# SBUF starting places of the fp32r operands in a two-layer DiT trunk: moving at 0 and weights at 64 modulo 128 bytes

## The chip, the core and the metric

The kernel runs on one core of one Trainium2 chip. The metric is device time in microseconds (us), the median of several executions of the same program. The engines are named as the profile names them: PE (TensorE matmuls), PEld (TensorE weight loads, which overlap PE), DVE (VectorE), ACT (ScalarE), POOL (GpSimd), SP (SyncE, which issues most of the DMAs). A matmul has a *moving* operand, which is streamed through the array, and *weights*, which are loaded into it before; both are read from SBUF.

## What is computed

Two layers of a diffusion transformer over 512 latent tokens of width 1024, with 256 context tokens. Layer 0 mixes with attention (four heads global, four heads with a window of 128 and a sink), layer 1 with a Fourier transform over channels and tokens; both end in a gated ConvFFN of width 2816 with a depthwise convolution of three taps. The parts that matter here, cut from the reference:

```python
def conv_ffn(h, w_up, conv_w, conv_b, w_down):
    u = h @ w_up
    up = jnp.pad(u, ((0, 0), (1, 1), (0, 0)))
    u = up[:, :-2] * conv_w[0] + up[:, 1:-1] * conv_w[1] + up[:, 2:] * conv_w[2] + conv_b
    gate, val = jnp.split(u, 2, axis=-1)
    return (jax.nn.silu(gate) * val) @ w_down
...
    for i in range(DEPTH):
...
        if i % 2 == 0:
            a = i // 2
            y, yc = attention_mixers(h, hc, attn_w_in[a], attn_w_out[a], q_norm_g[a], k_norm_g[a], sink[a],
                                     cos, sin, ctx_next)
        else:
            w_f = fourier_w_out[i // 2]
            y = fourier_mix(h) @ w_f
        x = x + g1 * rms_norm(y, norm_g[i, 1])
        h = modulate(rms_norm(x, norm_g[i, 2]), sh2, sc2)
        x = x + g2 * rms_norm(conv_ffn(h, ffn_w_up[i], ffn_conv_w[i], ffn_conv_b[i], ffn_w_down[i]), norm_g[i, 3])
```

## The kernel before

Almost every large product is made of three matmuls on fp32r tiles. `split` (line 124) turns an fp32 tile into a high part (ACT, a cast) and a low part (DVE or POOL, the difference), and `mm3` (lines 101 to 105) issues high times high, high times low and low times high into the same PSUM tile. So in the profile nearly all matmuls carry the lines L102, L103 and L104, and they are told apart by their tiles: `mm<-hl,wh` has `hl` moving and `wh` as weights. A matmul streams 256 or 512 columns (a few 258 or 384) against weights of 128 by 128.

The tiles that matter:

- `hh`, `hl` (8 x 512 columns): the current activations, high and low. They move in the projections of the FFNs; they are the weights in the attention projections and in the Fourier transform over channels.
- `wh`, `wl` (five buffers each, from `wpair`): the split weights of the matrix that is just being applied. In the projections that give tokens by channels they are the moving side.
- `xh`, `xl` (four buffers each, from `Pairs.pair`): mostly the gated FFN activations, which move in the down projections; at two places they hold weights instead (the output projection's last four blocks and the first up blocks of both FFNs).
- `zh`, `zl` (four buffers each, from `Pairs.spare`): the differences and sums of activation blocks that move in `seven_products`, a scheme of seven block products in place of eight; near the end of each FFN they hold weights of the down projection.
- `qh`, `ql`, `kh`, `kl`, `th`, `tl`: queries, keys and transposed probabilities in attention. `ch`, `cl`: the context's activations.
- `ct`, `Z`, `A`, `B`, `N`: the cosine table, the transformed activations and the outputs of the Fourier mixing. Rows of `ct`, `A` and `N` are 258 columns long.

Tiles live in pools. A pool lays them out in the order in which their names first occur, each rounded up to 32 bytes, and a new pool's tiles wait for the last users of whatever lay in their bytes before. So the starting place of a tile follows from the sizes of all tiles ahead of it, and the order of `mk` calls is also the order in SBUF. The instructions of each engine run in the order of the program; the order itself is set by the code and by priorities, not by places.

`rstd` (line 187) makes the reciprocal root of a mean square in small tiles `st_v`, `st_t`, `st_r`. `tables(0)` casts the first half of the cosine table, on ACT, during the boundary between the layers.

Of the kernel before, what the change touches and what calls it, by code (L numbers as in the profile page):

```python
# [10 lines left out]
F32 = mybir.dt.float32  # L11
F32R = mybir.dt.float32r
# [7 lines left out]
P = 128  # L20
D = 1024
KC = D // P
T = 512
TT = T // P
# [24 lines left out]
SWEEP = [3, 6]  # L49
GP = [1, 1]  # L50
BP = [4, 1]

WARM = 36
HOT = [5, 8, 5, 6]
# [25 lines left out]
def kernel(ctx: ExitStack, tc: tile.TileContext, a):  # L80
# [5 lines left out]
    def mk(pool, shape, dt=F32, tag=None, bufs=1):  # L86
        cnt[0] += 1
        n = nbufs.setdefault((id(pool), tag), (pool, bufs))[1]
        return pool.tile(shape, dt, tag=tag, name=f"{tag}_{cnt[0]}", bufs=n)
# [39 lines left out]
    cp = ctx.enter_context(tc.tile_pool(name="cp", bufs=1))  # L129
# [18 lines left out]
    ident = con[:, K_ID:K_ID + P]  # L148
    ones32 = mk(cp, [P, 32], F32, "ones32")
    V.memset(ones32, 1.0)  # L150
    eps = mk(cp, [P, 1], F32, "eps")
    once = mk(cp, [P, 1], F32, "once")
    V.memset(eps, EPS)
    mods = mk(cp, [P, 2, 6, KC], F32, "mods")
    der = mk(cp, [P, 2, 4, KC], F32, "der")
    scol = mk(cp, [P, 2, KC], F32, "scol")

    def ng(l, i):
        return cols[:, C_NG + (l * 4 + i) * KC:C_NG + (l * 4 + i + 1) * KC]
# [13 lines left out]
    W4 = HT // 4  # L173
# [12 lines left out]

    def rstd(ps):
        w = ps.shape[1]
        v, t, r = (mk(cp, [P, W4], F32, "st_" + c, 2)[:, :w] for c in "vtr")
        S.activation(out=r, in_=ps, func=AF.Abs_reciprocal_sqrt, bias=eps, scale=1.0 / D)  # L190
        V.tensor_scalar(out=v, in0=ps, scalar1=1.0 / D, scalar2=EPS, op0=ALU.mult, op1=ALU.add)
        V.tensor_tensor(out=t, in0=r, in1=r, op=ALU.mult)
        V.scalar_tensor_tensor(out=t, in0=t, scalar=-0.5, in1=v, op0=ALU.mult, op1=ALU.mult)
        V.scalar_tensor_tensor(out=v, in0=t, scalar=1.5, in1=r, op0=ALU.add, op1=ALU.mult)
        return v
# [351 lines left out]
    def out_weights(u, xp):  # L547
        r = raw([P, KC, 256], a["w_out"][u])
        ws = []
        for i in range(2):  # L550
            wh, wl = (xp.pair if u >= 2 else wpair)([P, KC, P])
            split(wh, wl, r[:, :, i * P:(i + 1) * P])
            ws.append([(wh[:, k, :], wl[:, k, :]) for k in range(KC)])
        return ws


    with ExitStack() as es:
# [7 lines left out]
        nsink = mk(ap, [P, 4], F32, "nsink")  # L565
        qst = mk(ap, [P, 2, TT, 2], F32, "qst")
        qtm = mk(ap, [P, 8], F32, "qtm")
        qrs = mk(ap, [P, 2, TT, 2], F32, "qrs")


        kh = mk(ap, [P, NK], F32R, "kh")
        kl = mk(ap, [P, NK], F32R, "kl")

        def keys(kv, parts):
            b0 = 0
# [512 lines left out]
        return ps, sl  # L1088


    class Pairs:
        def __init__(self, es):
            self.first = es.enter_context(tc.tile_pool(name="x0", bufs=1, reuse_waits="tile"))
# [7 lines left out]

        def spare(self, shape):
            return mk(self.pool, shape, F32R, "zh", 4), mk(self.pool, shape, F32R, "zl", 4)

    def up_weights(l, pairs, fis, eng=V):
        for fi in fis:
            r = raw([P, 2, KC, P], a["w_up"][l, fi])
            for i in range(2):
                wh, wl = pairs([P, KC, P])
                split(wh, wl, r[:, i, :, :], eng)  # L1110
                yield [(wh[:, k, :], wl[:, k, :]) for k in range(KC)]
# [120 lines left out]
    def ffn(l, xp, ready, pre, mid, gem, plain=None):  # L1232
# [69 lines left out]
        def begin(us):  # L1302
            for u in us:
                fi, i = divmod(u, 2)
                if u >= len(ready):
                    ready.extend(up_weights(l, xp.pair if u >= 4 and l == 0 else wpair, [fi]))
                first.append((fi, i, ready[u], mk(pps, [P, T], F32, "mm", 6) if plain is None or u < skew else None))

        def sweep(us, sl, ks=range(KC)):
# [69 lines left out]
        for gi, (f0, nch) in enumerate(GROUPS[l]):  # L1379
            end = gi == len(GROUPS[l]) - 1  # L1380
            for fi in range(max(f0, FIRST), f0 + nch):
                if fi == SUMS[l]:
                    bs = seven_inputs(xp)
                if fi in SEVEN[l]:
                    cc = [conv(fi, i, u, None, i == 1) for i, u in enumerate(seven_products(l, fi, pps, bs))]
                else:
                    cc = []
                    for i, w in enumerate(up_weights(l, wpair, [fi])):
                        ps = mk(pps, [P, T], F32, "mm", 6)
                        up_mm(ps, w, slice(0, T))  # L1390
                        cc.append(conv(fi, i, ps))
                gated(fi, cc[0], cc[1], f0)
                if l == 0 and fi not in SEVEN[l]:
                    pump(gem, GP[0])
                if l:
                    pump(down, DOWN.get(fi, 0))
            pump(down, 100)
            if l and end:
                xT = mk(cp, [P, KC, T], F32, "xT")
                SY.dma_start(out=xT, in_=away)  # L1400
            g_ = [gs[fi] for fi in range(f0, f0 + nch)]
            if l and not end:
                down = down_tiles(gi, nch, g_)
                pump(down)
                continue
            ws = {}

            def part(d, hs, ps=None):
                down_part(gi, ws[d], g_, d, hs, ps, end)

            def weights(d):
                ws[d] = down_weights(gi, nch, d, xp.spare if end and 4 <= d < 7 else wpair)


            hs = {d: [0, 1] if not end or d == 0 else [0] for d in range(KC)}
            begun = {}
            if end:
                pump(gem, 100)
                fence()
            keep = dict(fences)  # L1420
            fences.clear()
            for d in range(2):
                weights(d)
            fences.update(keep)
            for d in range(2):
                begun[d] = y_mm(pps, ws[d], g_, hs[d], False)[0]
            for d in range(KC):
                if d not in ws:
                    weights(d)
                part(d, hs[d], begun.get(d))  # L1430
                if gem is not None and not end:
                    pump(gem, GP[1])
            if end:
                mid(ys)
                for d in range(1, KC):
                    part(d, [1])
# [12 lines left out]
    with ExitStack() as es:  # L1449
        up = es.enter_context(tc.tile_pool(name="up", bufs=1, reuse_waits="tile", side="right"))  # L1450
        M1 = 258
        A = [mk(up, [P, 4, M1], F32R, "A%d" % i) for i in range(2)]
        B = [mk(up, [P, 4, 256], F32R, "B%d" % i) for i in range(2)]
        N = [mk(up, [4, M1], F32R, "N%d" % i) for i in range(2)]
        wk = es.enter_context(tc.tile_pool(name="wk", bufs=1, reuse_waits="tile", side="right"))
        zs = ExitStack()
        zp = zs.enter_context(tc.tile_pool(name="zp", bufs=1, reuse_waits="tile"))
        ft = wpair([P, 2, 256])
        st = wpair([P, TT, 256])
        ct = [mk(zp, [P, TT, M1], F32R, "ct%d" % i) for i in range(2)]  # L1460
        split(ft[0], ft[1], raw([P, 2, 256], a["dft_c"]), G)
        lc = raw([P, TT, M1], a["dft_lc"])
        ls = raw([P, TT, 256], a["dft_ls"])
        Z = [mk(zp, [P, TT, 4, 256], F32R, "Z%d" % i) for i in range(2)]


        def over_channels(g, h):
# [130 lines left out]
        group(3, [2, 3])  # L1598
        zs.close()
        xp = Pairs(ctx)  # L1600
        soon = up_weights_dma(1, xp.pair, [0, 1])

        ys = YStat(wk, 2)
        for d in range(KC):
# [140 lines left out]
```

## Time and profile before

| | |
|---|---|
| median of 3 runs | 1145.2 us (1142.97 to 1145.88) |
| span of the profiled execution | 1141.3 us |
| PE busy | 1113.0 us, 98% of the span |
| PEld busy | 965.9 us, 85% |
| DVE busy | 899.9 us, 79% |
| ACT busy | 595.6 us, 52% |
| POOL busy | 177.9 us, 16% |

The span runs from the first to the last instruction that the profile shows in one execution; the timed runs are 1.7 to 4.6 us longer. Matmuls are pipelined: the profile gives each a start and a modelled end, so one matmul's duration overlaps the next one's, and how fast PE goes is read from the distance between starts. Lines of the timeline view read: start in us, duration in us, engine, source line, operation, out<-in, shapes, count.

### The profile page before, as it was taken

To read this page: it belongs to the slowest core of one execution; us is meant where nothing else is said; L and a number is where in the kernel's file an instruction comes from. 1 tells how busy PE (TensorE), PEld (TensorE's weight loads), DVE (VectorE), ACT (ScalarE), POOL (GpSimd) and SP (SyncE) were. 2 spreads that over 40 slices of the span, in tenths; PEclk is the share of its full clock that TensorE was granted. 3 is DMA by queue.
4 is the path that set the end of the run, shared out by engine and by line. 5 is a ranking of instruction groups with operands and counts; after the bars stand their busy time and mean duration, and the time that the engine had idled before them with its cause. 6 is when DMAs were issued, how large, how long until landed. Compare 5 with 4: busy or idle time off the path is not lost.

```text
span 1141.3 us, 19565 instructions
## 1 busy us (share of the span) xinstructions
PE 1113.0 (98%) x7810; PEld 965.9 (85%) x7810; DVE 899.9 (79%) x1469; ACT 595.6 (52%) x1068; POOL 177.9 (16%) x180
## 2 busy tenths in 40 slices
PE   9999999999999999999999999999999999999995
PEld 5689888868898978887898898779888898899995
DVE  4678777765679976987999668978998998879755
ACT  4342355665665633552465446557746555555533
POOL 1236422421420000000000143620000000000012
PEclk9999999999999999999999999999999999999998
DMA  9675101075143355535534401742215533323332
GB/s 367 258 240 212 38 1 38 27 264 190 38 186 111 109 196 213 222 120 203 195 108 174 131 5 59 233 119 109 74 47 165 185 103 116 103 91 94 103 143 74
DMA packets 33763, 155.83 MB, mean 137 GB/s; under 512 B 3460, under 2 KB 8196, under 8 KB 22024
## 3 DMA queue, kind: packets, MB, share of 16 engines
q1 hardware_dynamic: 32520, 150.39, 37.0%
q0 software_dynamic: 1152, 4.19, 1.6%
q8 instruction: 61, 1.00, 0.3%
q14 instruction: 30, 0.25, 0.1%
HBM read 148.28 MB, written 6.29 MB: 135 GB/s over the span
## 4 chain that ended last, share of the span: by engine, by line
PE 83%; DVE 10%; ACT 3%; issue 2%; DMA 1%; POOL 1%; DVEq 0%; POOLq 0%; ACTq 0%; SPq 0%
PE mm L102 24%; PE mm L103 22%; PE mm L104 22%; DVE wl L125 2%; PE PT L950 1%; DVE md_t L302 1%; PE O L102 1%; PE gm L527 1%; DMA raw<-in_w_up 1%; PE O L103 1%; PE gm L102 1%; PE gm L104 1%; PE gm L103 1%; PE O L104 1%; PE mm L178 1%
## 5 line engine op out<-in xcount | busy, mean ns | idle before, releaser
L125 ACT CAST wh<-raw 128x1024 fp32r<-128x1024 f32 (+2 forms) x207 | 190.6, 933 | 169.8 <-PE mm L103 118.7
L125 DVE TENSOR_TENSOR wl<-raw,wh 128x1024 fp32r<-128x1024 f32 (+2 forms) x197 | 214.8, 1098 | 54.3 <-ACT wh L125 54.0
L102 PE MATMUL mm<-hh,wh 128*128 128x256 f32 (+1 forms) x632 | 206.4, 327 | 1.5 <-ACT yT L925 0.9
L104 PE MATMUL mm<-hh,wl 128*128 128x256 f32 (+1 forms) x632 | 203.7, 323 | 0.0
L103 PE MATMUL mm<-hl,wh 128*128 128x256 f32 (+1 forms) x632 | 203.5, 322 | 0.0
L277 POOL TENSOR_TENSOR gacc<-gacc,sq 128x256 f32<-128x256 f32 (+1 forms) x33 | 27.9, 847 | 717.0 <-ACT sq L275 716.2
L102 PEld LDWEIGHTS mm<-hh,wh 128*128 128x128 f32 x632 | 118.9, 188 | 17.7 <-ACT sq L1194 4.4
L103 PEld LDWEIGHTS mm<-hl,wh 128*128 128x128 f32 x632 | 118.9, 188 | 11.1
L104 PEld LDWEIGHTS mm<-hh,wl 128*128 128x128 f32 x632 | 118.9, 188 | 10.5 <-DVE wl L125 0.4
L102 PE MATMUL mm<-zh,wh 128*128 128x256 f32 x384 | 109.1, 284 | 1.4 <-ACT sq L1197 0.8
L102 PE MATMUL mm<-xh,wh 128*128 128x512 f32 (+1 forms) x302 | 107.5, 356 | 0.0
L103 PE MATMUL mm<-xl,wh 128*128 128x512 f32 (+1 forms) x302 | 106.8, 354 | 0.0
L103 PE MATMUL mm<-zl,wh 128*128 128x256 f32 x384 | 106.6, 278 | 0.0
L104 PE MATMUL mm<-zh,wl 128*128 128x256 f32 x384 | 106.4, 277 | 0.0
L104 PE MATMUL mm<-xh,wl 128*128 128x512 f32 (+1 forms) x302 | 106.2, 352 | 0.0
L102 PEld LDWEIGHTS mm<-zh,wh 128*128 128x128 f32 x384 | 72.3, 188 | 5.7 <-ACT sq L1197 4.4
L103 PEld LDWEIGHTS mm<-zl,wh 128*128 128x128 f32 x384 | 72.2, 188 | 0.0
L104 PEld LDWEIGHTS mm<-zh,wl 128*128 128x128 f32 x384 | 72.1, 188 | 0.0
L102 PEld LDWEIGHTS mm<-xh,wh 128*128 128x128 f32 x302 | 56.8, 188 | 9.9 <-issue 1.6
L103 PEld LDWEIGHTS mm<-xl,wh 128*128 128x128 f32 x302 | 56.8, 188 | 8.6 <-issue 0.4
L104 PEld LDWEIGHTS mm<-xh,wl 128*128 128x128 f32 x302 | 56.7, 188 | 8.6
L1255 ACT ACTIVATE cv<-mm,cols 128x512 f32<-128x512 f32 x59 | 45.9, 777 | 28.6 <-PE mm L104 22.2
(435 smaller groups left out, 2802.3 us busy)
## 6 DMA issues: line engine op xcount, KB each, us to landing
raw<-in_w_up SPq DMA_DIRECT2D x42, 1024.0 KB, 4.9
xT<-in_mod_r SPq DMA_DIRECT2D x20, 1024.0 KB, 5.2
raw<-in_w_down SPq DMA_DIRECT2D x32, 384.0 KB, 3.1
raw<-in_mod_p SPq DMA_DIRECT2D x8, 1024.0 KB, 4.9
raw<-in_w_down SPq DMA_DIRECT2D x16, 512.0 KB, 4.1
raw<-in_w_in SPq DMA_DIRECT2D x6, 1024.0 KB, 7.8
yT<-in_mod_r SPq DMA_DIRECT2D x10, 512.0 KB, 6.5
raw<-in_w_out SPq DMA_DIRECT2D x4, 1024.0 KB, 5.0
```

What stands on the lines that cost most here:

```text
L102: i = PE.matmul(out, lhsT=ah, rhs=bh, start=start, stop=False, skip_group_check=skip)
L103: PE.matmul(out, lhsT=ah, rhs=bl, start=False, stop=False, skip_group_check=skip)
L104: return i, PE.matmul(out, lhsT=al, rhs=bh, start=False, stop=stop, skip_group_check=skip)
L125: i = S.copy(out=h, in_=src), eng.tensor_tensor(out=l, in0=src, in1=f(h), op=ALU.subtract)
L178: PE.matmul(ps[:32, :src.shape[1]], lhsT=ones32, rhs=src, start=True, stop=True)
L277: G.tensor_tensor(out=self.acc[:, sl], in0=self.acc[:, sl], in1=sq[:, sl], op=ALU.add)
L302: m = V.scalar_tensor_tensor(out=t, in0=yT[:, k, hs], scalar=der[:, l, gi, k:k + 1], in1=R, op0=ALU.mult, op1=ALU.mult)
L527: PE.matmul(ps[32 * q:32 * q + 32, :], lhsT=spad[:, k, :], rhs=w[:, q * T:(q + 1) * T], start=k == 0, stop=k == KC - 1)
L950: PE.transpose(out=pt[:, j * P:(j + 1) * P], in_=Ps[j][:, off:off + P], identity=ident)
L1255: S.activation(out=cv, in_=ps, func=AF.Identity, bias=bc, scale=wc[1])
```

## The change

No instruction is added or taken away, no DMA and no amount of data changes. Tiles move in SBUF. Their starting places, in bytes modulo 128, as the two programs place them:

| tile | before | after |
|---|---|---|
| `hh`, `hl`, `xT` | 0 | 0 |
| `wh`, `wl` | 32 | 64 |
| `xh`, `xl` as moving side | 96 | 0 |
| `xh`, `xl` as weights | 96 | 64 |
| `zh`, `zl` as moving side | 96 | 0 |
| `zh`, `zl` as weights | 96 | 64 |
| `kh`, `kl` (moving) and `qh`, `ql` (weights) | 32 and 32 | 0 and 64 |
| `th`, `tl` (moving) | 96 | 0 |
| `ch`, `cl` (weights) | 96 | 0 |
| `ct` (moving), rows | 96 and 0, each row 8 further | 64, every row |
| `Z` (weights) | 32 | 0 |
| `A` (moving), rows | 96 and 0, each row 8 further | 0, every row |
| `B`, `N` (moving) | 32; 32 and 64 | 0 |

In the pairs of moving side and weights, the distance between the two places, modulo 128, was 32 or 96 for `hh` with `wh` or `xh`, and for `wh` with `hh`; 0 for `xh` with `zh`, `kh` with `qh`, `B` with `wh`, `wh` with `Z`; 64 for `zh` or `xh` with `wh`, `th` with `wh`, and `wh` with `ch`. After the change it is 64 in all of them. The two pairs of single columns (`sh`) are left out of this.

The core of the diff:

```diff
+SIDE = 16
...
+    scol = mk(cp, [P, 2, KC], F32, "scol")
     eps = mk(cp, [P, 1], F32, "eps")
     once = mk(cp, [P, 1], F32, "once")
+    mk(cp, [P, 8], F32, "cpad")
...
-    scol = mk(cp, [P, 2, KC], F32, "scol")
...
-        v, t, r = (mk(cp, [P, W4], F32, "st_" + c, 2)[:, :w] for c in "vtr")
+        v, t, r = (mk(cp, [P, W4], F32, "st_" + c, n)[:, :w] for c, n in (("v", 2), ("t", 1), ("r", 2)))
...
-            wh, wl = (xp.pair if u >= 2 else wpair)([P, KC, P])
+            wh, wl = (xp.weights if u >= 2 else wpair)([P, KC, P])
...
-        qrs = mk(ap, [P, 2, TT, 2], F32, "qrs")
-
-
         kh = mk(ap, [P, NK], F32R, "kh")
         kl = mk(ap, [P, NK], F32R, "kl")
+        qrs = mk(ap, [P, 2, TT, 2], F32, "qrs")
...
+    def beside(pool, shape, tag):
+        n, m = shape[1:]
+        return mk(pool, [P, 2 * SIDE + n * m], F32R, tag, 4)[:, SIDE:SIDE + n * m].rearrange("p (a b) -> p a b", b=m)
+
     class Pairs:
...
+        def weights(self, shape):
+            return [beside(self.first, shape, n) for n in ("xh", "xl")]
+
+        def spare_weights(self, shape):
+            return [beside(self.pool, shape, n) for n in ("zh", "zl")]
...
-                    ready.extend(up_weights(l, xp.pair if u >= 4 and l == 0 else wpair, [fi]))
+                    ready.extend(up_weights(l, xp.weights if u >= 4 and l == 0 else wpair, [fi]))
...
-                ws[d] = down_weights(gi, nch, d, xp.spare if end and 4 <= d < 7 else wpair)
+                ws[d] = down_weights(gi, nch, d, xp.spare_weights if end and 4 <= d < 7 else wpair)
...
-        A = [mk(up, [P, 4, M1], F32R, "A%d" % i) for i in range(2)]
         B = [mk(up, [P, 4, 256], F32R, "B%d" % i) for i in range(2)]
-        N = [mk(up, [4, M1], F32R, "N%d" % i) for i in range(2)]
+        A = [mk(up, [P, 4, 288], F32R, "A%d" % i)[:, :, :M1] for i in range(2)]
+        N = [mk(up, [4, M1 + 30], F32R, "N%d" % i)[:, :M1] for i in range(2)]
+        mk(up, [P, 24], F32, "upad")
...
-        ct = [mk(zp, [P, TT, M1], F32R, "ct%d" % i) for i in range(2)]
+        Z = [mk(zp, [P, TT, 4, 256], F32R, "Z%d" % i) for i in range(2)]
+        ct = [mk(zp, [P, 32 + TT * 288], F32R, "ct%d" % i)[:, SIDE:SIDE + TT * 288].rearrange(
+            "p (t m) -> p t m", t=TT)[:, :, :M1] for i in range(2)]
...
-        Z = [mk(zp, [P, TT, 4, 256], F32R, "Z%d" % i) for i in range(2)]
...
-        soon = up_weights_dma(1, xp.pair, [0, 1])
+        soon = up_weights_dma(1, xp.weights, [0, 1])
```

On PE, SP and POOL the instructions stand in the same order as before, and on ACT too. Two things move all the same. First, since the pool of `ct` and `Z` is laid out the other way round, the first half of the cosine table now lies over bytes that another tile used last. On ACT, in the boundary between the layers (`tables(0)`), before:

```order
586 L190 ACTIVATE st_r_7286<-misc_7279,eps_73 128x4 [waits PE_49]
587 L268 ACTIVATE cv_1051_7244<-yT_68 128x256 [waits DVE_49]
588 L125 CAST ct_1062_7267<-raw_7273 128x516 [waits DMAHW0_49]
589 L190 ACTIVATE st_r_7341<-misc_7322,eps_73 128x64 [waits PE_49]
590 L1484 ACTIVATE Z_1067_7277<-mm_7352,st_v_7284 128x256 [waits DVE_49,PE_49]
```

And now, the same five instructions:

```order
586 L193 ACTIVATE st_r_7288<-misc_7281,eps_74 128x4 [waits PE_49]
587 L271 ACTIVATE cv_1052_7245<-yT_68 128x256 [waits DVE_49]
588 L127 CAST ct_1066_7271<-raw_7277 128x2x258 [waits DMAHW0_49,PE_49,Activation_49]
589 L193 ACTIVATE st_r_7343<-misc_7324,eps_74 128x64 [waits PE_49]
590 L1498 ACTIVATE Z_1064_7269<-mm_7354,st_v_7286 128x256 [waits DVE_49,PE_49]
```

The cast of `ct` waits for PE too now: for the matmuls of L184 (L187 after) that read the second `cv` tile. Second, `st_t` has one buffer in place of two, and on DVE, where two reciprocal roots are interleaved at the start of layer 1's FFN, the order of two instructions is exchanged. Before:

```order
1021 L191 TENSOR_SCALAR st_v_8561<-mm_8133 128x64 [waits Activation_49]
1022 L194 SCALAR_TENSOR_TENSOR st_v_8471<-st_t_8472,st_r_8473 128x64 [waits DVE_49]
1023 L192 TENSOR_TENSOR st_t_8562<-st_r_8563 128x64
1024 L215 TENSOR_TENSOR Rs_8524<-st_v_8471,con_66 128x256 [waits DVE_49]
1025 L193 SCALAR_TENSOR_TENSOR st_t_8562<-st_t_8562,st_v_8561 128x64 [waits DVE_49]
1026 L194 SCALAR_TENSOR_TENSOR st_v_8561<-st_t_8562,st_r_8563 128x64 [waits DVE_49]
1027 L215 TENSOR_TENSOR Rs_8614<-st_v_8561,con_66 128x256 [waits DVE_49]
```

Now:

```order
1021 L194 TENSOR_SCALAR st_v_8563<-mm_8135 128x64 [waits Activation_49]
1022 L197 SCALAR_TENSOR_TENSOR st_v_8473<-st_t_8474,st_r_8475 128x64 [waits DVE_49]
1023 L218 TENSOR_TENSOR Rs_8526<-st_v_8473,con_66 128x256 [waits DVE_49]
1024 L195 TENSOR_TENSOR st_t_8564<-st_r_8565 128x64
1025 L196 SCALAR_TENSOR_TENSOR st_t_8564<-st_t_8564,st_v_8563 128x64 [waits DVE_49]
1026 L197 SCALAR_TENSOR_TENSOR st_v_8563<-st_t_8564,st_r_8565 128x64 [waits DVE_49]
1027 L218 TENSOR_TENSOR Rs_8616<-st_v_8563,con_66 128x256 [waits DVE_49]
```

The first spread of `Rs` comes one instruction earlier, the second root's first step one later.

## The prediction

> **What bounds the kernel now.** I read the page first: its busy times, and the chain that ended last.
>
> ```profile
> span 1141.3 us, 19565 instructions
> PE 1113.0 (98%) x7810; PEld 965.9 (85%) x7810; DVE 899.9 (79%) x1469; ACT 595.6 (52%) x1068; POOL 177.9 (16%) x180
> PEclk9999999999999999999999999999999999999998
> PE 83%; DVE 10%; ACT 3%; issue 2%; DMA 1%; POOL 1%; DVEq 0%; POOLq 0%; ACTq 0%; SPq 0%
> PE mm L102 24%; PE mm L103 22%; PE mm L104 22%; DVE wl L125 2%; PE PT L950 1%; DVE md_t L302 1%; PE O L102 1%; PE gm L527 1%; DMA raw<-in_w_up 1%; PE O L103 1%; PE gm L102 1%; PE gm L104 1%; PE gm L103 1%; PE O L104 1%; PE mm L178 1%
> ```
>
> PE carries 83% of the chain, and the three lines of `mm3` alone 68%. The granted clock is full all through, so the clock has nothing to give. What a matmul takes while PE is never idle is therefore worth 83% of itself at the end. The next view is the groups of instructions on PE, shapes apart (last two numbers ahead of the idle time: total us, mean ns of one).
>
> ```profile
> L103 PE MATMUL mm<-hl,wh 128*128 128x256 f32 x400 | 112.9, 282 | 0.0
> L104 PE MATMUL mm<-hh,wl 128*128 128x256 f32 x400 | 112.8, 282 | 0.0
> L103 PE MATMUL mm<-zl,wh 128*128 128x256 f32 x384 | 106.6, 278 | 0.0
> L104 PE MATMUL mm<-zh,wl 128*128 128x256 f32 x384 | 106.4, 277 | 0.0
> L103 PE MATMUL mm<-xl,wh 128*128 128x256 f32 x112 | 31.6, 282 | 0.0
> L104 PE MATMUL mm<-xh,wl 128*128 128x256 f32 x112 | 31.2, 279 | 0.0
> L103 PE MATMUL mm<-xl,zh 128*128 128x256 f32 x84 | 23.8, 283 | 0.0
> L103 PE MATMUL mm<-wl,hh 128*128 128x256 f32 x112 | 31.6, 282 | 0.0
> L103 PE MATMUL gm<-wl,hh 128*128 128x256 f32 x96 | 27.2, 283 | 0.0
> L103 PE MATMUL mm<-hl,wh 128*128 128x512 f32 x224 | 88.3, 394 | 0.0
> L104 PE MATMUL mm<-hh,wl 128*128 128x512 f32 x224 | 88.8, 396 | 0.0
> L103 PE MATMUL mm<-xl,wh 128*128 128x512 f32 x190 | 75.1, 396 | 0.0
> L104 PE MATMUL mm<-xh,wl 128*128 128x512 f32 x190 | 75.0, 395 | 0.0
> L103 PE MATMUL mm<-wl,ch 128*128 128x512 f32 x16 | 6.3, 391 | 0.0
> L104 PE MATMUL mm<-wh,cl 128*128 128x512 f32 x16 | 6.3, 393 | 0.0
> ```
>
> Matmuls of one shape do not take one time, and the table of places in the section on the change sorts them: at 256 columns 278 and 277 where the places are 64 apart (`zh` with `wh`), 282 where they are 32 apart (`hh` with `wh`, `wh` with `hh`), 283 where they are equal (`xh` with `zh`). Durations contain a fixed part, so I check them on starts. The timeline of PE in one down projection gives the first and the last matmul of a run of 51 with `xh` and `wh`, and of the run of 72 with `xh` and `zh` that follows at once; then two rows of a weight load beside the matmul ahead of it; then first and last of a run of 96 with `hh` and `wh`, and of eleven 512-column matmuls with `wh` and `ch`.
>
> ```profile
> 646.11 0.28 PE L102 MATMUL mm<-xh,wh 128*128 128x256 f32 x1
> 651.78 0.28 PE L104 MATMUL mm<-xh,wl 128*128 128x256 f32 x1
> 651.90 0.28 PE L102 MATMUL mm<-xh,zh 128*128 128x256 f32 x1
> 660.41 0.28 PE L104 MATMUL mm<-xh,zl 128*128 128x256 f32 x1
> ...
> 654.89 0.28 PE L103 MATMUL mm<-xl,zh 128*128 128x256 f32 x1
> 654.90 0.19 PEld L104 LDWEIGHTS mm<-xh,zl 128*128 128x128 f32 x1
> ...
> 335.00 0.28 PE L102 MATMUL mm<-hh,wh 128*128 128x256 f32 x1
> 346.39 0.28 PE L104 MATMUL mm<-hh,wl 128*128 128x256 f32 x1
> ...
> 49.09 0.39 PE L103 MATMUL mm<-wl,ch 128*128 128x512 f32 x1
> 51.38 0.39 PE L104 MATMUL mm<-wh,cl 128*128 128x512 f32 x1
> ```
>
> Start to start: 5.67 us over 50 steps is 113 ns, 64 apart; 8.51 over 71 is 120 ns, equal; 11.39 over 95 is 120 ns, 32 apart. So a duration is the step plus about 163 ns, and differences of durations are differences of steps. The first two runs share engine, stage, shape and moving tile; only the weights' place differs. The weight load starts within 0.01 us of the matmul ahead of it, so the two reads run side by side, and it is this pair that the change moves.
>
> [...]
>
> **The change part by part.** *256 columns.* The level at 64 apart is not always 113 ns: `xh` with `wh` has 282 and 279 beside the 278 and 277 of `zh`. Weighted by their counts, (768 x 277.5 + 224 x 280.5) / 992 = 278.2. I bring every other 256-column row to this mean: it is the same distance, and the nearest row there is. `hh` with `wh`, 1,200 matmuls (three lines of 400), 282 - 278.2: 4.6 us. `hh` with `xh`, 384 of them, also 32 apart, the same 3.8 ns: 1.5. `wh` with `hh`, 336 and 288 in `mm` and `gm`, 3.8: 2.4. `xh` with `zh`, 252 by 4.8: 1.2. The smaller groups of 256, 258 and 384 columns (`A`, `B`, `ct`, `Z`, the scores), some 680 by the counts of the same view, by 4 ns, an estimate from these rows: 2.7. Together 12.4 us. Bounds: nothing, if 0 and 64 are no better than 0 and 32; and 113 ns for all 4,800, the old 64-apart ones too, which adds 1.8 ns each, or 8.6 us.
>
> *512 columns.* Here 64 apart is seen twice and the two disagree: `xh` with `wh` (96 and 32) has 396 and 395, as much as the 394 and 396 of `hh` with `wh`; `wh` with `ch` (32 and 96) has 391 and 393, 3 ns less, and its run steps at 2.29 / 10 = 229 ns. The new places, 0 and 64 or the reverse, are equally far from both, so I take the middle, 1.5 ns on all 1,722 matmuls of this width: 2.6 us. Bounds: nothing, and 229 ns everywhere (395 is a step of 232 to 233, so some 4 ns each, 6.9 us).
>
> Sum on PE: 15.0 us, of which 83% stands on the chain: 12.4 us.
>
> *What does not get through.* The windows view (us; then busy time of each engine with its count) shows two stretches in which DVE has no room.
>
> ```profile
> 330.00:352.00 22.00, 22.00 (x187) 22.00 (x186) 21.65 (x30) 19.20 (x32) 2.45 (x3) 1.00 0.41 149
> 352.00:380.00 28.00, 28.00 (x143) 23.42 (x142) 27.80 (x35) 13.90 (x20) 0.00 (x0) 1.00 0.23 87
> 380.00:640.00 260.00, 259.98 (x1529) 222.45 (x1528) 218.45 (x270) 125.40 (x188) 0.00 (x0) 1.00 0.48 171
> 920.00:1100.00 180.00, 179.75 (x1212) 161.95 (x1211) 149.58 (x198) 95.43 (x147) 0.00 (x0) 1.00 0.33 110
> ```
>
> In the first two DVE is busy 21.65 of 22 and 27.80 of 28 us. What PE gains there (187 by 3.8 ns, 143 by about 2) I strike out whole: 1.0 us. In the third and fourth, which hold 2,741 of the matmuls, DVE is busy 84% and 83%, so the gain of a few us has room there.
>
> *The new wait.* The cast of `ct` ran on ACT at 687.41, ahead of the `st_r` that PE's sums release.
>
> ```profile
> 687.41 0.61 ACT L125 CAST ct<-raw 128x516 fp32r<-128x516 f32 x1
> 688.65 0.32 ACT L190 ACTIVATE st_r<-misc,eps 128x64 f32<-128x64 f32 x1 [0.64 <-PE misc L184]
> 688.07 0.52 PE L184 MATMUL misc<-cv,ones 128*32 128x64 f32 x24
> 694.59 0.28 PE L102 MATMUL mm<-ct,Z 128*128 128x258 f32 x1
> ```
>
> It now waits for some of these 24 small matmuls, which end at 688.59. So the cast takes about 688.6 to 689.1, and `st_r`, queued behind it, starts 0.4 us late. Behind `st_r` come the root, the spread and DVE's update of the second half, which PE waits for: 0.4 us on the path, at worst the cast's whole 0.61, at best nothing if PE still has first-half products to do. POOL's low part of `ct` comes as late, and `ct` is first read only at 694.6.
>
> *The rest at nothing.* Exchanging two small DVE instructions leaves DVE's sum as it was; with one `st_t` buffer reader and writer are both on DVE, in order. Were that cover gone, it would cost one small instruction, 0.3 us. The moved DMAs into `xh` wait for PE a few matmuls later, under 1 us, while POOL, which issues them, is still busy ahead of them. That DVE, ACT or DMA should mind a shift by 32 bytes no row suggests: the same 128x256 operation, DVE's L360 on `hl` (place 0) and L1485 on `Z` (place 32), takes equal time.
>
> ```profile
> 694.81 0.48 DVE L360 SCALAR_TENSOR_TENSOR hl<-xT,der,hh 128x256 fp32r<-128x256 f32 x1
> 693.36 0.48 DVE L1485 SCALAR_TENSOR_TENSOR Z<-mm,st_v,Z 128x256 fp32r<-128x256 f32 x1
> ```
>
> **Sum.** 12.4 - 1.0 - 0.4 = 11.0 us off the span of 1141.3: 1130.3. The timed runs lie 1.7 to 4.6 us above this span, and what lies around it is not touched, so I take the 11.0 off the median: 1145.2 - 11.0 = 1134.
>
> **The rivals.**
>
> *Everything falls to the best rows.* If 0 and 64 always give 113 ns at 256 and 229 at 512 columns, PE saves 12.4 + 8.6 + 6.9 = 27.9, of which 83% less 1.4 is 21.8: 1123; a step of 226 at 512 columns, an estimate as twice 113, is three further ns on 1,722 and makes it 1119. For: the rows show these levels. Against: 64 apart has both levels today, in `xh` with `wh` even within one tile pair.
>
> *No change.* The levels belong to stages and their neighbours, not to places; PE's steps stay, and the time is 1145. [...] Against: the 113 and 120 ns back to back at 651.8. For: 512 columns, where 64 apart in `xh` is as slow as 32 apart in `hh`.
>
> *Half gets through.* Other engines' waits take the freed time outside the two stretches as well: some 5.5 us, 1139.5. Against: the DVE shares of 84% and 83%.
>
> *Slower.* What counts is where the moving side starts, not the distance. `hh`, the main moving side that starts at 0 today, never shows less than the 282 of its row. If moving at 0 means 282 whatever the weights, the 1,152 products of `zh` rise from 277.5 and the 336 of `xh` from 280.5: 5.2 + 0.5 us, nearly all on the chain, with no gain elsewhere, and the 0.4 us of the cast: 1151. It decides once the 64-apart mean of the new places lies above 281 ns, where gain and loss at 256 columns cancel. Against: with `xh` moving at one place, 32 and 96 for the weights give 113 and 120 ns.
>
> **How the numbers follow.** Chances: the forecast 0.50, with 1128 to 1140 as its own range from the unknown 512-column level; the best rows 0.23; half 0.10; no change 0.10; slower 0.07. About 0.3%, or 3.4 us, is what a measurement of this kernel can tell from no change. The forecast, the best rows and most of the half case lie beyond it: 0.79 faster, 0.14 within, 0.07 slower. The range goes from 1119, the bound of the best rows, to 1145, no change; above it lies the slower case, below it what no row shows.
>
> **What would show it.** In the profile after, `hl` with `wh` and `xl` with `zh` at 256 columns should fall from 282 and 283 to 276 to 279, and `zl` with `wh` stay at 276 to 278; 512 columns should show 390 to 395. PE's matmul count stays 7810, the chain keeps PE above 80%, and `ct`'s cast stands at about 688.6 minus what was gained by then. I am wrong in the main step if `hl` with `wh` keeps 282, and wrong in the carrying if steps fall and DVE's or ACT's share of the chain grows by as much.

## The result, and the profile after

The changed kernel took 1137.96 us (median of 4 executions, 1137.78 to 1138.46), the kernel before 1145.13 beside it (4 executions, 1142.97 to 1145.88). The ratio is 0.9946, with a 95% interval of 0.9932 to 0.9960: 7.2 us by the medians, 6.2 by the ratio. The direction of the forecast and its range hold; of the forecast 11.0 us a little more than half came.

The page of the changed kernel: its span, the busy times, the granted clock, and the shares of the chain that ended last.

```profile
span 1136.0 us, 19565 instructions
PE 1105.1 (97%) x7810; PEld 962.1 (85%) x7810; DVE 902.3 (79%) x1469; ACT 595.4 (52%) x1068; POOL 174.6 (15%) x180
PEclk9999999999999999999999999999999999999998
PE 77%; DVE 14%; ACT 5%; DMA 2%; issue 2%; POOL 1%; DVEq 0%; POOLq 0%; ACTq 0%; SPq 0%
```

PE is busy 7.9 us less with the same 7810 matmuls, the span is 5.3 us shorter, and on the chain PE has lost 6 points to DVE (10 to 14%) and ACT (3 to 5%). So PE did get faster, and part of what it gained is now spent waiting.

The groups of PE, shapes apart (total us, mean ns of one; the lines of `mm3` are now L104 to L106):

```profile
L105 PE MATMUL mm<-hl,wh 128*128 128x256 f32 x400 | 112.1, 280 | 0.0
L105 PE MATMUL mm<-zl,wh 128*128 128x256 f32 x384 | 107.1, 279 | 0.0
L106 PE MATMUL mm<-zh,wl 128*128 128x256 f32 x384 | 107.0, 279 | 0.0
L105 PE MATMUL mm<-xl,zh 128*128 128x256 f32 x84 | 23.5, 280 | 0.0
L105 PE MATMUL mm<-wl,hh 128*128 128x256 f32 x112 | 31.4, 280 | 0.0
L106 PE MATMUL mm<-hh,wl 128*128 128x512 f32 x224 | 88.0, 393 | 0.1
L105 PE MATMUL mm<-hl,wh 128*128 128x512 f32 x224 | 87.6, 391 | 0.0
L105 PE MATMUL mm<-xl,wh 128*128 128x512 f32 x190 | 74.7, 393 | 0.0
```

`hl` with `wh` went from 282 to 280 and not to 278; `xl` with `zh` from 283 to 280; `zl` and `zh` with `wh`, which were 64 apart before and after, got slower, 278 and 277 to 279. The 512-column rows fell by 3 ns (`hh` with `wl` 396 to 393, `hl` with `wh` 394 to 391), the double of the middle value I had taken.

The timeline of PE gives the runs that the prediction measured, first and last matmul of each: `hh` with `wh`, then `xh` with `wh`, then `xh` with `zh`.

```profile
334.09 0.28 PE L104 MATMUL mm<-hh,wh 128*128 128x256 f32 x1
...
344.86 0.28 PE L106 MATMUL mm<-hh,wl 128*128 128x256 f32 x1
...
642.97 0.28 PE L104 MATMUL mm<-xh,wh 128*128 128x256 f32 x1
...
648.87 0.28 PE L106 MATMUL mm<-xh,wl 128*128 128x256 f32 x1
648.98 0.28 PE L104 MATMUL mm<-xh,zh 128*128 128x256 f32 x1
...
657.33 0.28 PE L106 MATMUL mm<-xh,zl 128*128 128x256 f32 x1
```

96 products of `hh` now step at 10.77 / 95 = 113 ns (120 before). But 51 of `xh` with `wh` step at 5.90 / 50 = 118 ns, where they had 113, and 72 of `xh` with `zh` at 8.35 / 71 = 118 ns, where they had 120. All three are 64 apart modulo 128. Modulo 128 is not the whole rule.

To go on I use steps: the start of the next product less the start of this one, for each fp32r product whose successor has its width, joined with the addresses of both operands as the built program places them (the traces hold no addresses). Steps above 136 ns (256 columns) or 242 ns (512) are left out as waits. The distance is the start of the moving operand less that of the weights, **modulo 256**.

### The profile page after: what moved, and what is told of

Same layout as the page of the kernel before. It is cut to its first block, busy times and chain, and to the rows that moved or that the text cites. A ratio compares the mean times of both kernels' runs of the same rounds, so it can differ in the third digit from the quotient of the medians.

```text
span 1136.0 us, 19565 instructions
## 1 busy us (share of the span) xinstructions
PE 1105.1 (97%) x7810; PEld 962.1 (85%) x7810; DVE 902.3 (79%) x1469; ACT 595.4 (52%) x1068; POOL 174.6 (15%) x180
## 3 DMA queue, kind: packets, MB, share of 16 engines
q0 software_dynamic: 1152, 4.19, 1.6%
## 4 chain that ended last, share of the span: by engine, by line
PE 77%; DVE 14%; ACT 5%; DMA 2%; issue 2%; POOL 1%; DVEq 0%; POOLq 0%; ACTq 0%; SPq 0%
PE mm L104 21%; PE mm L106 20%; PE mm L105 20%; DVE wl L127 2%; PE PT L951 1%; DMA raw<-in_w_up 1%; DVE md_t L305 1%; PE O L104 1%; PE O L105 1%; PE gm L530 1%; PE gm L104 1%; PE gm L106 1%; ACT wh L127 1%; PE gm L105 1%; PE O L106 1%
## 5 line engine op out<-in xcount | busy, mean ns | idle before, releaser
L104 PE MATMUL mm<-hh,wh 128*128 128x256 f32 (+1 forms) x632 | 204.8, 325 | 1.9 <-ACT yT L926 0.9
L106 PE MATMUL mm<-hh,wl 128*128 128x256 f32 (+1 forms) x632 | 202.0, 320 | 0.4 <-DVE wl L127 0.2
L104 PEld LDWEIGHTS mm<-hh,wh 128*128 128x128 f32 x632 | 118.7, 188 | 17.0 <-ACT sq L1206 4.6
L106 PEld LDWEIGHTS mm<-hh,wl 128*128 128x128 f32 x632 | 118.7, 188 | 10.2 <-DVE wl L127 1.2
L104 PE MATMUL mm<-zh,wh 128*128 128x256 f32 x384 | 109.5, 285 | 1.2 <-ACT sq L1209 0.6
L104 PE MATMUL mm<-xh,wh 128*128 128x512 f32 (+1 forms) x302 | 107.1, 355 | 0.0
L106 PE MATMUL mm<-zh,wl 128*128 128x256 f32 x384 | 107.0, 279 | 0.0
L106 PE MATMUL mm<-xh,wl 128*128 128x512 f32 (+1 forms) x302 | 106.2, 352 | 0.0
L104 PEld LDWEIGHTS mm<-zh,wh 128*128 128x128 f32 x384 | 72.1, 188 | 5.5 <-ACT sq L1209 4.2
L106 PEld LDWEIGHTS mm<-zh,wl 128*128 128x128 f32 x384 | 72.5, 189 | 0.0
L104 PEld LDWEIGHTS mm<-xh,wh 128*128 128x128 f32 x302 | 56.7, 188 | 9.4 <-issue 1.6
L106 PEld LDWEIGHTS mm<-xh,wl 128*128 128x128 f32 x302 | 56.8, 188 | 8.0
```

The costliest lines, as they stand in the source:

```text
L104: i = PE.matmul(out, lhsT=ah, rhs=bh, start=start, stop=False, skip_group_check=skip)
L106: return i, PE.matmul(out, lhsT=al, rhs=bh, start=False, stop=stop, skip_group_check=skip)
```

## The experiments

One table for all of them; the text below tells what each was for. "PE" is the sum of the changes of those fp32r steps that hold no wait in either profile, against the first profile of the kernel before, in us. The two mean steps are over all products of that width.

| kernel | time, median (executions) | ratio to before, 95% interval | 256 columns, ns | 512 columns, ns | PE, us |
|---|---|---|---|---|---|
| before, again | 1144.46 (1) | - | 117.6 | 233.2 | +0.1 |
| after | 1137.96 (4) | 0.9946 (0.9932 to 0.9960) | 116.4 | 230.2 | -9.5 |
| after, again | 1138.23 (6) | 0.9958 (0.9942 to 0.9974) | 116.5 | 230.2 | -9.2 |
| wh32 | 1141.03 (11) | 0.9975 (0.9966 to 0.9984) | 116.8 | 232.3 | -4.4 |
| wh64 | 1138.92 (5) | 0.9958 (0.9945 to 0.9971) | 117.8 | 229.0 | -5.7 |
| all32 | 1138.46 (5) | 0.9953 (0.9940 to 0.9965) | 116.2 | 230.2 | -10.1 |
| hh128 | 1137.85 (6) | 0.9952 (0.9939 to 0.9965) | 115.9 | 232.1 | -8.4 |
| x_equal | 1139.23 (5) | 0.9959 (0.9947 to 0.9971) | 116.3 | 229.9 | -10.2 |
| pad_only | 1138.85 (6) | 0.9959 (0.9944 to 0.9973) | 116.9 | 230.9 | -6.2 |
| best | 1138.41 (6) | 0.9949 (0.9935 to 0.9963) | 116.2 | 230.0 | -10.5 |
| ct_first | 1138.07 (6) | 0.9945 (0.9925 to 0.9965) | 116.5 | 230.2 | -9.0 |

The first profile of before has 117.5 and 233.25 ns.

**The changed kernel once more** (after, again). No edit.

> The changed kernel as it is, profiled and timed once more. After the change the 256-column runs sit at one of two steps, 113 or 118 ns start to start, although all are 64 apart (hh with wh 113.3 ns at 334 us, wh with hh 117.8 ns at 72 us). Theory A, the level is set by the program (its order and places): the same stretches show the same level again, and the mean of all 256-column steps is 116.4 ns within 0.3. Theory B, the level is set by the phase in which a run happens to begin, which DMA arrivals change from one execution to the next: several of the stretches change level, and the mean moves by up to 1 ns. Time 1138 within 1 us by both.

The means come out at 116.5 and 230.2 ns against 116.4 and 230.2, and the kernel before, profiled again, at 117.6 and 233.2 against 117.5 and 233.25. The two stretches named keep their levels, and theory A holds for the means. It does not hold for every stretch: of 4,001 products of 256 columns at distance 64, 313 change between the lower level (115 ns or less) and the upper one from one execution of this program to the other. In the kernel before, the 48 products of `wh` with `ch` at 101 us step at 113.3 ns in its first profile and at 117.8 in its second. So the means have a cause in the program, while a single stretch can also change level by chance.

**Only `wh` and what lies behind it, by 32 bytes** (wh32).

```
+    mk(wp, [P, 8], F32, "wpad")
     def raw(shape, src):
```

> Only one tile of 32 bytes is added ahead of raw, wh and wl, so wh, wl and everything behind them lie 32 bytes further on. hh with wh, wh with hh, hh with xh and xT with wh are 32 apart again (as before the change, on the other side: 0 and 96), some 3,600 products; zh, xh, ch, kh with their partners stay 64 apart, now at 32 and 96. Theory distance: hh with wh goes from 117.0 to about 119.3 ns a step at 256 columns, wh with hh from 115.8 to 118.3, hh with xh from 114.5 to 118, and at 512 columns from 229 to 233.3, while zh with wh and xh with zh stay where they are: 1224 x 2.3 + 672 x 2.5 + 384 x 3.5 + 912 x 4 ns = 9.5 us, of which some 70% to 80% reaches the end: 1144 to 1146. Rival, the places themselves matter (moving at 0 or weights at 64 is good): zh and xh change too. Rival, the gain did not come from the pairs of a product at all: 1138.

The products of `hh` at 512 columns went back to 233.1 ns, `wh` with `hh` to 118.2; `zh` with `wh`, still 64 apart, moved by less than 1 ns. Of the 5.1 us of PE that are lost, 512 columns make 3.5. But `hh` with `wh` at 256 columns stayed at 117.1 where 119.3 was expected: 32 bytes above the weights is not the same as the 96 above (160 below) that the kernel before had. The time rose, by less than expected: 1141.0, neither 1138 nor 1144.

**The same with 64 bytes** (wh64). `[P, 16]` in place of `[P, 8]`.

> The same with 64 bytes: the same some 3,600 products have both operands at place 0 (distance 0), the others stay 64 apart at 64 and 0. Theory distance: at 256 columns hh with wh, wh with hh and hh with xh go to the 120 ns that xh with zh showed at distance 0 before the change: 1224 x 3.0 + 672 x 4.2 + 384 x 5.5 = 8.6 us; at 512 columns no row shows distance 0, so between the 233.3 ns of distance 32 (3.9 us on 912) and twice 120 ns (10 us); together 12 to 19 us, of which 70% to 80% at the end: 1147 to 1153, slower than the kernel before. Rival, not the pairs: 1138.

Half a miss, and the most useful one. At 256 columns equal places are as bad as expected: `hh` with `wh` 119.0, `wh` with `hh` 119.5, `hh` with `xh` 119.7 at distance 0. At 512 columns they are the best of all: 227.3 ns. The groups of PE in this kernel show it in durations, 282 as before the change at 256 columns, and 390 at 512:

```profile
L105 PE MATMUL mm<-hl,wh 128*128 128x256 f32 x400 | 113.0, 282 | 0.0
L105 PE MATMUL mm<-hl,wh 128*128 128x512 f32 x224 | 87.3, 390 | 0.0
```

So in these runs the best distance depends on the number of columns. Against the kernel after, 256 columns lose 5.9 us and 512 columns win 2.0, PE is 3.8 us slower, and the time is 1 us longer: 1138.9, where 1147 to 1153 were expected.

**Everything by 32 bytes** (all32).

```
     con = mk(cp, [P, K_ALL], F32, "con")
+    mk(cp, [P, 8], F32, "front")
```

> A tile of 32 bytes ahead of xT: all tiles on the left side shift together, so all pairs stay 64 apart except the 216 products of A, B and N, which are placed from the other side and come to 32 apart; the places are now 32 for the moving side and 96 for the weights, or the reverse. Theory distance: 256-column steps stay at 116.4 within 1 ns, 512-column steps at 230.2 within 1, time 1138 to 1139.5. Rival, the absolute places matter: by the rows of before with 32 and 96, 256 columns go to 115.1 and 512 columns to 233.2; that is -1.3 x 4,356 and +3.0 x 1,722 ns, which nearly cancel in the time (1137 to 1139), so the steps decide.

116.2 and 230.2 ns, 1138.5 us: for the means, distances count, not places.

**The sign of the distance** (hh128). In the kernel after, one padded tile of `xh` and `zh` is 4,224 bytes, so its buffers begin in turn at 128 and at 0 modulo 256, while `wh` stays at 192. The same instructions of the same stage then have distance -64 and +64 side by side. That gave the next theory; the test moves `hh` alone:

```
     con = mk(cp, [P, K_ALL], F32, "con")
+    scol = mk(cp, [P, 2, KC], F32, "scol")
+    eps = mk(cp, [P, 1], F32, "eps")
+    mk(cp, [P, 8], F32, "cpad")
...
-    scol = mk(cp, [P, 2, KC], F32, "scol")
-    eps = mk(cp, [P, 1], F32, "eps")
...
-    mk(cp, [P, 8], F32, "cpad")
```

> Three small tiles move from behind hl to ahead of xT, so xT, yT, hh and hl lie 128 bytes further on and nothing else moves: every pair keeps its places modulo 128, but for all products with hh the sign of the distance modulo 256 turns over. Theory modulo 256: in the kernel after, products of xh and zh at 256 columns step at 115.6 to 116.4 ns where the moving operand starts 64 below its weights and at 117.7 to 118.0 where it starts 64 above (modulo 256), and at 512 columns the other way round, 232 to 234 below and 228.5 to 230 above. So hh with wh should fall from 117.0 to about 115.6 at 256 columns and rise from 229 to about 232.5 at 512, and wh with hh rise from 115.8 to about 117.8: -1224 x 1.4 + 672 x 2 + 720 x 3.5 ns = +2.2 us on PE, 1139 to 1140.5. Rival, modulo 128 is all that counts and the levels differ by stage: steps stay at 117.0, 115.8 and 229, time 1138.

`hh` with `wh` fell to 115.2 ns at 256 columns and rose to 233.2 at 512; `wh` with `hh` rose from 115.8 to 116.8 at 256 and fell from 233.4 to 229.3 at 512. These four turned as the theory says. One pair did not: `hh` with `xh` at 256 columns has 114.1 ns at -64 and 115.1 at +64 in the kernel after, and here 114.1 and 113.9. The groups of this kernel (after: 280 and 391):

```profile
L106 PE MATMUL mm<-hh,wl 128*128 128x256 f32 x400 | 111.4, 279 | 0.2 <-DVE wl L127 0.2
L105 PE MATMUL mm<-hl,wh 128*128 128x512 f32 x224 | 88.4, 395 | 0.0
```

PE lost 1.1 us against after instead of the expected 2.2, and the time shows no loss: 1 us is below what these timings resolve.

All kernels together give this table of mean steps in ns (d is the distance modulo 256; the pairs are `hh` moving with `wh`, `wh` moving with `hh`, `zh` with `wh`, `xh` with `wh`):

| d | 256: hh,wh | 256: wh,hh | 256: zh,wh | 512: hh,wh | 512: wh,hh | 512: xh,wh |
|---|---|---|---|---|---|---|
| 0 | 119.0 | 119.5 | - | 227.3 | 229.6 | 228.8 |
| +32 | 117.1 | - | - | 233.1 | - | - |
| +64 | 117.1 | 116.8 | 117.8 | 229.1 | 229.3 | 229.6 |
| +96 | 119.3 | - | - | 233.4 | - | - |
| 128 | - | - | - | - | - | 232.0 |
| -96 | - | 118.3 | - | - | 234.0 | - |
| -64 | 115.2 | 115.8 | 115.7 | 233.2 | 233.4 | 232.3 |
| -32 | - | 118.2 | - | - | 233.2 | - |

A cell is the mean in one kernel; the cells at -64 and 256 columns vary between kernels by up to 1.5 ns (`zh` with `wh` 114.8 in the kernel before, 116.3 in the one with the pad alone), the others by 1.3 ns at most.

At 256 columns such a mean is not the step of each run. In the kernel after there are 63 runs of at least 12 products of `hh` with `wh`, all at +64: seven step at 113 to 114 ns, the others at 117 to 120. (The run of 96 at 334 us, shown above, is one of the seven.) The runs at -64 split in the same way. Over all profiles 52% of the steps at -64 are 115 ns or less, and 19% of those at +64. So here the distance sets how often the lower level comes up; what chooses the level of one run stays open, and a modulus of 2048 in place of 256 does not sort these runs (17 to 22% of the products lie at the lower level at each of its four distances). At 512 columns the runs of `hh` with `wh` in the kernel after all lie between 228.9 and 229.2 ns.

**512-column products of the down projections at equal places** (x_equal).

```
-            return mk(self.first, shape, F32R, "xh", 4), mk(self.first, shape, F32R, "xl", 4)
+            n, m = shape[1:]
+            return [mk(self.first, [P, 2 * SIDE + n * m], F32R, t, 4)[:, at:at + n * m].rearrange(...)
...
-    ... else xp.pair([P, 2, T])
+    ... else xp.pair([P, 2, T], 0 if f0 == GROUPS[l][-1][0] else SIDE)
```

> Only the places of the xh and xl that move at 512 columns in the down projections (528 products) are changed, by 64 bytes, so that they start at the same place modulo 128 as wh (half of them modulo 256 too). Theory, at 512 columns distance 0 is best: their steps go from 232 (below) and 229 (above) to the 227 to 228 ns that hh with wh shows at distance 0, 528 x 3.5 ns = 1.8 us on PE, of which 60% to 80%: 1136.5 to 1137. Rival, the 227 ns belongs to hh, or needs the same place modulo 256: half of these products or all stay at 229 to 232, and the time at 1138. The 256-column steps do not change by either.

The rival was right for half of them: at distance 0 modulo 256 the steps are 228.8, at 128 they are 232.0. Together 230.3 against 231 before the edit, a gain of 0.4 us on PE, and none that the time shows.

**How much the 32 bytes ahead of `wh` do alone** (pad_only). In the kernel before:

```
     once = mk(cp, [P, 1], F32, "once")
+    mk(cp, [P, 8], F32, "cpad")
```

> The kernel before with a single tile of 32 bytes behind once, ahead of wh: wh at 64, xh, zh, ch at 0 as after the change, but no padded rows and no side pads, and the tables keep their order. hh with wh, wh with hh are 64 apart as after; xh and zh with wh stay 64 below; hh with xh and xh with zh are at equal places. Theory of the pairs: hh with wh 119.3 to 117.0, wh with hh 118.3 to 115.8, at 512 columns hh with wh and xT with wh 233.3 to 229; zh with wh stays at 115, xh with wh at 512 columns at 233; hh with xh goes from 118 to 119: 2.8 + 1.7 + 3.9 - 0.4 = 8.0 us on PE against some 10 after, 1139 to 1140. If the side pads and padded rows carried the gain: 1143 to 1145.

PE gains 6.2 us (8.0 were expected), and the time is 1138.85, which the interval does not tell from the full change. The largest miss, 1.6 us, is `zh` with `wh`, which stays at -64 and was expected to stay at 115 ns: it went from 114.9 to 116.3. The rest of the change (side pads, padded rows, the order of some tiles) adds 3.3 us on PE and nothing at the end that these timings resolve.

**The edit of x_equal, a shift of `zh` and `zl`, and the order of `ct`** (best), and then **the order alone** (ct_first). The order is the move of one line:

```
-        Z = [mk(zp, [P, TT, 4, 256], F32R, "Z%d" % i) for i in range(2)]
         ct = [mk(zp, [P, 32 + TT * 288], F32R, "ct%d" % i)...
+        Z = [mk(zp, [P, TT, 4, 256], F32R, "Z%d" % i) for i in range(2)]
```

> The edit of x_equal, and two more: zh and zl as moving tiles start 128 bytes on in every second buffer, so that all of them start 64 below wh modulo 256 (240 products, 117.8 to 115.6 ns: 0.5 us), and Z is placed behind ct again, at the same places modulo 256, so that the cast of ct need not wait for the sums of cv (0.4 us at 688 us). Theory: 1.8 + 0.5 us on PE at 60% to 80%, and 0.4: 1135.8 to 1136.5. In the profile the products behind 690 us should no longer come 0.4 us later against the kernel before than those ahead of it. Rival, the freed time goes to waits on other engines: 1138.

> The changed kernel with Z placed behind ct again instead of ahead of it, at the same places modulo 256, so that the cast of ct on ACT need not wait for the sums of cv. Theory, the new wait costs 0.4 us: the cast stands at about 684.4 instead of 685.6 us, st_r follows the sums at once, and against the kernel before the products behind 692 us come no later than those at 680 us (after: 0.4 us later). Time 1137.5 within 1.5. Rival, ACT's order hides it: no change at 692 us.

In the first of the two, the shift of `zh` half missed: the products of `zh` with `wh` that it took from +64 to -64 went from 117.8 to 116.7 ns, where 115.6 was expected.

For the order, the timeline of ACT, first in the kernel after, then in the kernel with only this line moved:

```profile
685.60 0.62 ACT L127 CAST ct<-raw 128x516 fp32r<-128x516 f32 x1 [0.93 <-ACT cv L271]
686.12 0.31 ACT L193 ACTIVATE st_r<-misc,eps 128x64 f32<-128x64 f32 x1
```

```profile
684.38 0.61 ACT L127 CAST ct<-raw 128x516 fp32r<-128x516 f32 x1
685.60 0.31 ACT L193 ACTIVATE st_r<-misc,eps 128x64 f32<-128x64 f32 x1 [0.61 <-PE misc L187]
```

The cast goes back by 1.2 us and `st_r` starts 0.52 us earlier. PE's steps with waits between 684 and 700 us, against the kernel before, cost 0.54 us in after, -0.16 in this kernel and 0.17 in the one with all three edits: the new wait costs 0.4 to 0.7 us. The combined kernel has the shortest profiled span of all, 1133.9 us, and its time, 1138.4, is not told apart from that of after. So no version here is shown to beat the change.

**The kernel before once more** (before, again). No edit.

> The kernel before as it is, profiled once more. Two things differ between its first profile and those of the kernels with the change and are tested here. At 47.7 us the two instructions md_t from xT took DVE 0.48 us each in the kernel before, and 1.53 us each beside POOL's subtraction wl in all eight profiles with wh at another place, which makes PE's products 0.9 us later. If that is tied to the change, this profile shows 0.48 again; if it is chance, it may show 1.53. Between 718 and 724 us the granted clock fell to half in five of those eight profiles and not in the first one of before; the same program (the kernel after) shows it once with and once without, so by chance theory it can appear here.

The first of the two came out as chance: here `md_t` took 1.52 us twice in the kernel before too, and PE lost the same 0.9 us. (The profiles with `wh` at another place were nine, not eight.) The drop of the clock is not in this profile; the last section returns to it. First the kernel after, DVE and POOL; then DVE and POOL in the first profile of before; then this profile of before (all from their timelines):

```profile
47.73 2.97 DVE L238 SCALAR_TENSOR_TENSOR md_t<-xT,derc,Rs 128x256 f32<-128x256 f32 x2
```

```profile
47.63 1.34 POOL L127 TENSOR_TENSOR wl<-raw,wh 128x512 fp32r<-128x512 f32 x1 [10.57 <-ACT wh L127]
```

```profile
47.66 0.88 DVE L235 SCALAR_TENSOR_TENSOR md_t<-xT,derc,Rs 128x256 f32<-128x256 f32 x2
```

```profile
47.57 4.10 POOL L125 TENSOR_TENSOR wl<-raw,wh 128x512 fp32r<-128x512 f32 x1 [10.59 <-ACT wh L125]
```

```profile
47.87 2.97 DVE L235 SCALAR_TENSOR_TENSOR md_t<-xT,derc,Rs 128x256 f32<-128x256 f32 x2
```

Either POOL's subtraction takes 4.10 us and DVE's pair 0.88, or 1.34 and 2.97 (POOL's second subtraction then stands beside DVE's second instruction): where the one is short, the other is long. What decides which of the two is long, these rows do not show: POOL's row starts 0.1 us ahead of DVE's in both cases (47.57 and 47.66 us, 47.63 and 47.73). The first profile of before had the outcome that is better for PE, and of all profiles only this one had it. Against the second profile of before the difference of spans is 1142.7 - 1136.0 = 6.7 us.

## Why the prediction was right, and where not

**The mechanism was right.** The steps do depend on the places. Moving tiles by 32, 64 or 128 bytes, with no other edit, moves the mean steps of most pairs whose distance it changes (`hh` with `wh` at 512 columns from 229.1 to 233.1 ns in wh32, to 227.3 in wh64, to 233.2 in hh128), moving everything by 32 bytes leaves the means of both widths (116.2 and 230.2 in all32, 116.4 and 230.2 in after), and the same program gives the same means again (116.5 and 230.2). It was not complete: the 120 ns of `xh` with `zh` were those of distance 0, but the 113 ns ahead of them were one of two levels at -64, as the kernel before shows at the same distance: 21 products of `xh` with `wh` at 643 us step at 117.8 ns, and the next 51 at 113.4. And pairs whose distance an edit leaves alone can drift, by up to 1.4 ns at 256 columns (`zh` with `wh` in pad_only). The 227.3 and 233.1 ns at 512 columns differ by nothing but 32 bytes in where `wh` and what lies behind it start (wh64 and wh32).

**The 256-column term was the wrong step.** I wrote that I bring every other 256-column row to the mean of the rows that were 64 apart, "it is the same distance". It is not: those rows (`zh`, `xh` with `wh`) were at -64, and the change put `hh` with `wh` at +64. Worked out per pair from the steps of before and after:

- `hh` with `wh`, 119.3 to 117.1 on 1,200: 2.6 us (forecast 4.6).
- `hh` with `xh`, 118.0 to 114.6 on 384: 1.3 (1.5).
- `wh` with `hh`, 118.3 to 115.8 on 624: 1.6 (2.4).
- `xh` with `zh`, 120.0 to 116.9 on 252: 0.8 (1.2).
- The small groups: at 258 columns 120.5 to 120.1 and at 384 no change, so some 0.2 (2.7, an estimate that nothing bore out).
- `zh` with `wh`, 114.8 to 116.1 on 1,152, and `xh` with `wh`, 115.8 to 116.9 on 336: 1.9 lost (forecast nothing). About half of this stands at the other sign, to which the side pads took part of the buffers; the other half at -64 itself, where `zh` with `wh` rose from 114.9 to 115.7.

Together 4.6 us where 12.4 were forecast; the mean step gives as much (1.1 ns on 4,356 products, 4.8 us).

**The 512-column term was too small.** The two levels whose middle I took, 233 for `xh` with `wh` and 229 for `wh` with `ch`, looked like a disagreement at one distance. They are -64 and +64. The change put `hh` with `wh` at +64, where its step fell from 233.4 to 229.1, and half of `xh` too: together 233.25 to 230.2 on 1,722 products, 5.3 us for 2.6 forecast and 6.9 as the bound. That more came than forecast was luck: nothing in the prediction chose the sign.

**The sum on PE** is then 10 us for 15. The missing sign explains the 512-column error and 2.0 us of the 7.8 missing at 256 columns (`hh` with `wh`, which hh128 brings to 115.2 ns). The small groups make 2.5, `zh` and `xh` with `wh` 1.9, of which the sign gives about half; the rest is spread over the other pairs. The two errors go opposite ways, which kept the sum nearer than its parts.

**What got through.** Counting only products that wait in neither profile, PE saved 9.5 us in the kernel after; 3.9 us of that went to steps with waits. I had struck out 1.0 us for two stretches in which DVE has no room. In the first, PE took 1.0 us less for its products without a wait; in the second, 0.8 us of waits came in. The two stretches in the kernel after:

```profile
330.00:352.00 22.00, 22.00 (x189) 21.73 (x188) 21.66 (x30) 19.14 (x32) 1.85 (x3) 1.00 0.39 145
352.00:380.00 28.00, 27.76 (x146) 23.49 (x145) 28.00 (x36) 13.96 (x20) 0.00 (x0) 1.00 0.28 97
```

In the second, DVE is now busy 28.00 of 28 us, and PE has its first idle time there. The wait of the `ct` cast took 0.5 (forecast 0.4), the DVE and POOL order at 47 us 0.9 (chance, not forecast), and 130 to 330 and 790 to 920 us together 1.2, where the view of waits names DVE and ACT. So the 83% for the rest were too many. But most of the miss lies in the sum: with 10 us in place of 15, the same 83% less 1.4 would have given 6.9. "Half gets through", held at 0.10, has nearly the measured number (5.5), but it was reckoned on 15 us of PE. In the profiled executions the pad alone saves 6.2 us on PE with 1.9 us of waits, the full change 9.5 with 3.9, the combined kernel 10.5 with 3.0; the three median times lie within 1 us. My sign for it, PE's share of the chain above 80%, failed: 77% in after and 82% with the pad alone.

**The slower rival** (moving at 0 is bad whatever the weights) is refuted by the shift of everything by 32 bytes (116.2 ns at 256 columns with moving at 32, 116.4 with moving at 0). **Best rows everywhere** cannot be had with one distance: none in the table is best at both widths.

My range for `hl` with `wh` and `xl` with `zh`, 276 to 279, was missed by 1 ns (280 both); 390 to 395 at 512 columns held. **The cast of `ct`** stands at 685.60, as said: 688.6 less the 3.0 us gained by then.

## What to carry to other kernels

When rows of one shape differ by a few ns, sort them by the start addresses of both operands, with sign and with a larger modulus than the first that fits; two rows that "disagree" at one distance are a reason to look for the next bit, not to take a middle. Do it per width: the distance that was best for 256 columns was among the worst for 512 (-64, with 115.2 and 233.2 ns for `hh` with `wh`). Look at single runs too, not only at means: a mean can hide two levels (here near 113 and near 118 ns). Ask what room the next engine has before counting on a few per mille of the bounding one: here 3.9 of the 9.5 us that PE saved went to waits. Try the cheapest part of such a change alone: here one pad of 32 bytes brought 6.2 of the 9.5 us on PE, and a time of 1138.85 us against 1137.96.

## What the runs showed of the hardware that was not expected

In these runs the mean step of back-to-back fp32r products depends on the distance of the two operands modulo 256 and on the width: 114 to 120 ns at 256 columns, 227 to 234 at 512. At 256 columns and a distance of 64 it is a mixture of two levels, near 113 and near 118 ns. Why the sign turns between the widths, and what chooses the level, stays open; the traces show no record of the two reads.

The granted clock fell to half (0.50) in the middle of some executions. The windows view of two executions of the same program (after; columns as above, the clock stands ahead of the DMA share), the second one behind 718 us:

```profile
718.00:719.00 1.00, 1.00 (x7) 0.73 (x7) 1.00 (x3) 0.00 (x0) 1.00 (x3) 1.00 0.92 287
719.00:720.00 1.00, 1.00 (x11) 1.00 (x10) 1.00 (x3) 0.00 (x0) 1.00 (x1) 1.00 0.91 258
720.00:721.00 1.00, 1.00 (x11) 1.00 (x10) 1.00 (x1) 0.37 (x1) 1.00 (x1) 1.00 1.15 410
```

```profile
718.00:719.00 1.00, 1.00 (x6) 0.86 (x7) 1.00 (x3) 0.00 (x0) 1.00 (x2) 0.84 1.05 303
719.00:720.00 1.00, 1.00 (x7) 1.00 (x7) 1.00 (x3) 0.00 (x0) 1.00 (x1) 0.50 0.92 283
720.00:721.00 1.00, 1.00 (x6) 1.00 (x6) 0.85 (x1) 0.00 (x0) 0.81 (x1) 0.50 1.06 377
```

Six or seven products a microsecond instead of eleven, for some 3 us; between 700 and 730 us this execution loses 1.5 us more than the first, and the profiles of wh32, hh128 and ct_first lose some 3. Six of the twelve profiles have such a drop. It follows a stretch in which PE waits, but that alone does not decide: from 715 to 718.5 us PE is busy 2.63 of 3.5 us in the execution without the drop and 2.87 in the one with it. What sets the drop off, the traces do not show. The spread of the times goes with the clock. The six profiled executions with the drop have a mean clock of 0.993 to 0.995, the six without 0.996 or 0.997. Of the timed ones, the kernel before has a median of 1143.4 us in 26 executions at 0.996 or more, and 1145.5 in 13 below; the kernel after has 1137.8 in 6, and 1139.8 in 4. At the higher clock the change is worth 5.6 us, the pad alone 5.0 (1138.35 in 4).
